# Gated-delta layer: the scan's matmuls laid over the whole TensorE array, and its reciprocal roots taken with GpSimd's power operation

## The chip, the cores and the metric

One core of one Trainium2 chip runs the whole program. The metric is the device time of one execution in microseconds (us). The core has a matrix engine (TensorE, PE in the profile, with PEld for its weight loads), VectorE (DVE), ScalarE (ACT), GpSimd (POOL), and queues that issue DMAs (SP is SyncE's). Each engine has a list of its own instructions and takes them in that order.

## The reference, cut to what matters

Two layers run over 1024 prompt frames and 64 sample frames (1088 columns, 17 chunks of 64). The first is a gated convolution with band attention and is not touched. The second is a gated DeltaNet with 8 heads of width 128. For each chunk it computes

```
def l2norm(x):
    return x * lax.rsqrt(jnp.sum(x * x, axis=-1, keepdims=True) + EPS)
...
u = sol[..., :HD_C] - jnp.einsum('bhlk,bhkv->bhlv', sol[..., HD_C:], S)
qk = jnp.einsum('blhd,bmhd->bhlm', q, k) * decay
o = jnp.einsum('blhk,bhkv->blhv', q * jnp.exp(gc)[..., None], S) + jnp.einsum('bhlm,bhmv->blhv', qk, u)
S_new = jnp.exp(g_last)[..., None, None] * S + jnp.einsum('blhk,bhlv->bhkv', k_dec, u)
```

S is a 128x128 state per head. It goes from chunk to chunk, so the chunks of a head are a chain. sol comes from a triangular solve inside the chunk and does not need S. The output o is normalized per head by the reciprocal root of its mean square, multiplied by silu(z) and projected.

## The kernel before

Heads are worked on in four pairs p = 0 to 3. The 64 rows of a chunk of one head of the pair lie in partitions 0 to 63, those of the other in 64 to 127. A pair's 17 chunks go in three batches of 6, 6 and 5. For each batch there are these steps:

- `prepare` (L947) transposes k and q of each chunk on TensorE (tile `tr`), squares and sums them on ScalarE (L976, `junk`), takes the reciprocal roots `rr` of the sums on VectorE by a bit trick and three Newton steps (`rsqrt`, L773), scales with them (`sT`, `sA`, `kap`, L985 to L987), and reads the products of k with k and of k with q out of PSUM into `An` and `KQD` (L997, L998). `kt` is a copy of the transposed k, `kd` that k times a decay.
- `substitute` (L1010) inverts 16x16 blocks on GpSimd in 28 small operations (`px`, `AL`) between two DMAs through DRAM; `join` (L1030) brings the blocks together with 32-wide matmuls; `solve` (L1098) writes the solved values over v (`vt`) and over k (in `kq`).
- `scan` (L1124) is the chain over chunks. Per chunk it makes `ks`, the products of k and of q with S; adds v to give `us`; makes `su`, the product of `kd` with `us`; updates S (L1185); and in `outputs` (L1132), one chunk later, makes the product of `KQD` with `us`, adds the q part (`qs`, L1173) and sums squares.
- `finish` (L1196) takes the reciprocal root for up to four chunks of output, with three VectorE operations before it, two for the bit trick and twelve GpSimd operations for Newton, and one VectorE operation behind (L1200 to L1204); it scales the outputs (L1206), transposes and stores them to DRAM.

Beside this chain TensorE runs the layer's projections: `pjt`, 128x384 or 128x320, three matmuls for each block of 128 rows because operands are split into a high and a low part (`project`, L175). For pairs 0 to 2 these are the projections and convolutions of the next pair; during the last pair's scan they are the eight gate tiles (`gate`, L847); then comes the output projection `out`.

TensorE's order is written by hand. Each step is a generator that issues its matmuls and then yields a waiting time in estimated ns; `Order.run` (L88) keeps an estimated clock, moved on by every matmul (`mm`, L115), and always takes the ready step of best rank, scan first and the projections last. The other engines' orders come from the tile framework's scheduler. PSUM tiles `tr` and `su` have two banks each, `ks` one. The layout that the change touches is `kq`: the pair's k of both heads, then its q of both, as [2, 17, 2, 64] in the free dimension (`new_kq`, L833). Each float32 matmul is two records in the trace, a transpose or a `pjt` matmul one.

The 64-row operands make TensorE use parts of its array: `ks` is four matmuls of 64 output rows (trace: 128*64), `su` two with 64 contraction rows (64*128), the output two of 64*64. `pjt`, the transposes, and `solve` use all of it (128*128).

Of the kernel before, what the change touches and what calls it, by code (L numbers as in the profile page):

```python
# [107 lines left out]
class Net:  # L108
# [651 lines left out]
    def odd(self):  # L760
# [12 lines left out]
        def rsqrt(out, x, tmp, eng):  # L773
            dve.tensor_scalar(out.bitcast(I32), x.bitcast(I32), 1, None, ALU.logical_shift_right)
            dve.tensor_scalar(out.bitcast(I32), out.bitcast(I32), -1, 0x5F3759DF, ALU.mult, ALU.add)  # L775
            for _ in range(3):
                if eng is dve:
                    dve.scalar_tensor_tensor(tmp, out, -0.5, x, ALU.mult, ALU.mult)
                    dve.tensor_tensor(tmp, tmp, out, ALU.mult)
                    dve.scalar_tensor_tensor(out, tmp, 1.5, out, ALU.add, ALU.mult)  # L780
                else:
                    pool.tensor_tensor(tmp, out, out, ALU.mult)  # L782
                    pool.tensor_tensor(tmp, tmp, x, ALU.mult)
                    pool.tensor_scalar(tmp, tmp, -0.5, 1.5, ALU.mult, ALU.add)
                    pool.tensor_tensor(out, out, tmp, ALU.mult)

# [46 lines left out]
        def new_kq(p):  # L833
            KQ[p] = k1.tile([P, 2, NCH, 2, 64], F32, name="kq", tag="kq", bufs=2)
# [4 lines left out]
        def conv_dst(p, i):  # L839
            q = i % 2  # L840
            if i < 2:
                return 8 + 2 * p + q, KQ[p][:, 0, :, q, :]
            if i < 4:
                return 2 * p + q, KQ[p][:, 1, :, q, :]
            return 16 + 2 * p + q, V[p][:, :, q, :]
# [27 lines left out]
        def gates(ba):  # L873
            for n in ("beta", "egc", "dec", "gc"):
                G[n] = comp(n)
            beta, egc, dec, gc = (G[n] for n in ("beta", "egc", "dec", "gc"))
            buf = G["buf"] = k1.tile([P, NCH * P], F32, name="dbuf", tag="vt", bufs=2)
            x, ab, gg = (buf[:, 68 * i:68 * i + 68].rearrange("p (a c) -> p a c", c=NCH) for i in range(3))
# [22 lines left out]
            for j, c0 in enumerate((C_U, C_BD, C_H, C_H + 1)):  # L901
                w = cst[:, c0:c0 + P] if j < 2 else cst[:, c0:c0 + 1].broadcast_to([P, P])
                self.mm(ps[:, 68 * j:68 * j + 68], w, gf)
            gcf = gc.rearrange("p a c -> p (a c)")
# [5 lines left out]
            act.activation(egl.rearrange("p q a c -> p (q a c)"), ps[:, 136:272], AF.Exp)  # L910
            yield 1500
# [30 lines left out]
        def zeroed():  # L942
            for name, w in (("Cb", 32), ("BD", P)):
                Z[name] = self.kp.tile([P, NBM, w], F32, name=name)
                pool.memset(Z[name], 0.0)

        def prepare(p, b):  # L947
# [16 lines left out]
            ss = self.kp.tile([P, 2, NBM], F32, name="ss", tag="ss", bufs=2)[:, :, :nb]  # L964
            rr = self.kp.tile([P, 2, NBM], F32, name="rr", tag="rr", bufs=3)[:, :, :nb]
            tmp = self.kp.tile([P, 2, NBM], F32, name="rt", tag="rt", bufs=2)[:, :, :nb]
            junk = self.kp.tile([P, P], F32, name="junk", tag="junk", bufs=1)
            for i0 in range(0, nb, 4):
                m = min(4, nb - i0)
                for a in range(2):  # L970
                    ps = pst("tr").rearrange("p (c j) -> p c j", j=P)
                    for i in range(m):
                        c = c0 + i0 + i
                        self.tr(ps[:, i, :], kq[:, a, c].rearrange("p q t -> p (q t)"))
                    for i in range(m):
                        act.activation(junk, ps[:, i, :], AF.Square, accum_out=ss[:, a, i0 + i:i0 + i + 1])  # L976
                    if a == 0:
                        act.copy(out=kt[:, i0:i0 + m, :], in_=ps[:, :m, :])
                        dve.tensor_tensor(kd[:, i0:i0 + m, :], ps[:, :m, :],
# [384 lines left out]
```

## Time and profile before

| what | value |
|---|---|
| median of 3 runs | 1439.04 us (1437.8 to 1440.11) |
| the profiled execution's own time | 1441.69 us |
| its span, first to last instruction | 1439.9 us |
| ScalarE, share of the span | 676.3 us, 47% |
| second layer with scan and solve steps, from the first `tr` tile | from about 678 us |
| first and last `ks` matmul | 793.4 and 1287.4 us |
| mean granted TensorE clock | 0.982 of full |

The profile shows one execution. A group row gives busy time, mean ns of one record, then the idle time of the engine just before, with what ended it. A wait row gives who waited for whom: total us, how often, the longest. A timeline row gives start us, length us, the instruction and how many records are merged. TensorE's lengths overlap, since matmuls are pipelined: what one costs is read from the distance between starts.

### The profile page before, as it was taken

Reading aid. Unit: us, or ns where it says so; the run is one execution under the profiler, and the core shown is the slowest. Engines: PE = TensorE matmul, PEld = TensorE weight load, DVE = VectorE, ACT = ScalarE, POOL = GpSimd, SP = SyncE. Lnnn points to the kernel's source line nnn. Section 1 sums busy time; section 2 is a strip of 40 time slices with the busy share of each in tenths; the row PEclk is TensorE's granted clock in tenths of the full one; section 3 lists DMA queues with packets and bytes.
Section 4 is the critical chain, followed back from the end, with each engine's and each line's share of the span. In section 5 each row is a group of like instructions: output and inputs, shape, how many; then the busy total and the mean of one; then the engine's idle time right before and its main releaser. Section 6 shows DMA issues by size and latency. Waiting matters only on the chain. (4 is left out here: it accounts for less than half of the span.)

```text
span 1439.9 us, 28413 instructions
## 1 busy us (share of the span) xinstructions
PE 1367.9 (95%) x10600; PEld 1231.2 (86%) x10600; DVE 867.4 (60%) x2496; ACT 676.3 (47%) x1776; POOL 304.9 (21%) x805
## 2 busy tenths in 40 slices
PE   8999999999999999899889999999898989999996
PEld 6989998998999899788768777778786778889995
DVE  7675257237425754777787768666765765433554
ACT  7643345144334455676445554545443534333652
POOL 4001000000100014321235325140524151410222
PEclk9999999999999999999988999999999999999998
DMA  8403111210211274541433112121311142336753
GB/s 267 138 17 90 57 53 45 87 53 27 78 58 47 65 237 140 174 165 38 110 83 67 42 40 70 31 60 33 68 34 42 39 99 61 104 107 219 228 198 117
DMA packets 113834, 132.73 MB, mean 92 GB/s; under 512 B 35280, under 2 KB 80792, under 8 KB 113696
## 3 DMA queue, kind: packets, MB, share of 16 engines
q1 hardware_dynamic: 82448, 104.32, 24.8%
q10 hardware_dynamic: 31248, 26.60, 5.7%
q8 instruction: 83, 1.36, 0.4%
q14 instruction: 55, 0.45, 0.1%
HBM read 99.71 MB, written 34.31 MB: 93 GB/s over the span
## 5 line engine op out<-in xcount | busy, mean ns | idle before, releaser
L119 PE MATMUL pjt<-hhi,wlo 128*128 128x384 f32 (+1 forms) x1768 | 616.9, 349 | 2.8 <-DVE wlo L165 2.8
L119 PE MATMUL pjt<-hhi,whi 128*128 128x384 f32 (+1 forms) x1768 | 583.7, 330 | 10.0 <-ACT whi L164 4.8
L119 PE MATMUL pjt<-hlo,whi 128*128 128x384 f32 (+1 forms) x1768 | 575.9, 329 | 1.0 <-DVE hlo L418 0.9
L119 PEld LDWEIGHTS pjt<-hhi,wlo 128*128 128x128 f32 x1768 | 337.1, 191 | 27.0 <-issue 11.9
L119 PEld LDWEIGHTS pjt<-hhi,whi 128*128 128x128 f32 x1768 | 337.2, 191 | 16.6 <-ACT whi L164 5.8
L119 PEld LDWEIGHTS pjt<-hlo,whi 128*128 128x128 f32 x1768 | 335.5, 190 | 1.9 <-DVE hlo L418 1.9
L165 DVE TENSOR_TENSOR wlo<-wf,whi 128x512 fp32r<-128x512 f32 x222 | 152.5, 710 | 165.4 <-ACT whi L164 164.1
L164 ACT CAST whi<-wf 128x512 fp32r<-128x512 f32 x222 | 130.1, 619 | 166.9 <-PE pjt L119 122.4
L639 ACT ACTIVATE pr<-pr,mx 128x640 f32<-128x640 f32 (+5 forms) x72 | 50.9, 707 | 89.4 <-DVE mx L638 88.8
L811 DVE SCALAR_TENSOR_TENSOR kq<-pjt,par,kq 128x384 f32<-128x384 f32 (+2 forms) x144 | 71.6, 497 | 2.9
L600 POOL MEMSET bias<- 64x64 f32 x8 | 1.5, 182 | 320.7 <-DMA bias<-Gd 295.5
L375 POOL TENSOR_TENSOR sqa<-sqa,sq 128x384 f32<-128x384 f32 (+1 forms) x36 | 39.9, 1109 | 138.0 <-ACT sq L372 137.9
L636 DVE CUSTOM_DVE_ANT_0 pr<-sc,bias 128x640 f32<-128x640 f32 (+5 forms) x72 | 47.9, 666 | 26.8 <-PE sc L119 25.9
L1022 POOL TENSOR_TENSOR px<-AL 48x14 f32<-48x14 f32 (+6 forms) x168 | 46.1, 274 | 61.0 <-DMA AL<-Sd 52.0
L1185 DVE SCALAR_TENSOR_TENSOR S<-S,egl,su 128x128 f32<-128x128 f32 x128 | 40.6, 342 | 30.0 <-PE su L119 29.6
L782 POOL TENSOR_TENSOR so<-so 128x4 f32<-128x4 f32 (+2 forms) x72 | 17.1, 238 | 176.0 <-DVE so L775 117.6
L976 ACT ACTIVATE junk<-tr 128x128 f32<-128x128 f32 x136 | 37.7, 277 | 34.0 <-PE tr L124 28.9
L1023 POOL TENSOR_TENSOR AL<-AL,px 48x14 f32<-48x14 f32 (+6 forms) x168 | 46.2, 275 | 9.4
L124 PE MATMUL pt<-cst,pr 128*128 128x128 f32 (+1 forms) x280 | 43.3, 270 | 4.4 <-DVE pr L641 2.9
L1144 ACT ACTIVATE junk<-o 128x128 f32<-128x128 f32 x68 | 21.0, 309 | 50.8 <-DVE o L1140 40.9
L119 PE MATMUL pjt<-mhi,whi 128*128 128x384 f32 x128 | 43.0, 336 | 1.1 <-ACT whi L164 1.1
L119 PE MATMUL pjt<-mhi,wlo 128*128 128x384 f32 x128 | 43.0, 336 | 0.5 <-DVE wlo L165 0.5
(257 smaller groups left out, 2192.0 us busy)
## 6 DMA issues: line engine op xcount, KB each, us to landing
wf<-in_w_in SPq DMA_DIRECT2D x128, 256.0 KB, 3.7
wf<-in_w_out SPq DMA_DIRECT2D x96, 256.0 KB, 3.2
mf<-mixd SPq DMA_DIRECT2D x31, 192.0 KB, 4.5
x<-in_x SPq DMA_DIRECT2D x8, 384.0 KB, 5.8
xg<-in_x SPq DMA_DIRECT2D x2, 1536.0 KB
xd<-xg SPq DMA_DIRECT2D x2, 1536.0 KB
Dd<-dbuf ACTq DMA_DIRECT2D x16, 192.0 KB, 3.6
od<-o ACTq DMA_DIRECT2D x12, 256.0 KB, 2.3
```

The lines of the kernel that those rows point to most:

```text
L119: return self.pe.matmul(out, lhsT=lhsT, rhs=rhs, start=start, stop=stop, **k)
L124: return self.pe.transpose(out, in_, self.ident[0:k, 0:k])
L164: self.act.copy(out=hi, in_=x)
L165: (eng or self.dve).tensor_tensor(lo, x, hi.bitcast(F32), ALU.subtract)
L375: pool.tensor_tensor(acc, acc, sq, ALU.add)
L636: dve.tensor_tensor_reduce(out=cut(pr[0:nq, :nk]), in0=sc[0:nq, :nk // nw, :nw], in1=cut(b["bias"][a][0:nq, j0:j0 + nk]), scale=1.0, scala ...
L639: act.activation(pr[0:nq, :nk], pr[0:nq, :nk], AF.Exp, bias=mx[0:nq, 1:2], scale=1.0, accum_out=mx[0:nq, 2:3])
L811: dve.scalar_tensor_tensor(oi, ch(ps[:, i0 + j + 1:i0 + j + 1 + m]), cw[j], oi, ALU.mult, ALU.add)
L976: act.activation(junk, ps[:, i, :], AF.Square, accum_out=ss[:, a, i0 + i:i0 + i + 1])
L1022: pool.tensor_tensor(t, AL[:, j + 1:16, j:j + 1].broadcast_to([lanes, m, w]), x.broadcast_to([lanes, m, w]), ALU.mult)
L1023: pool.tensor_tensor(o, o, t, ALU.add)
L1185: dve.scalar_tensor_tensor(Sn[:, q, :], S[:, q, :], egl[:, q, p, c:c + 1], su[q], ALU.mult, ALU.add)
```

## The change

`kq` becomes [17, 4, 64]: per chunk k of head 0, q of head 0, q of head 1, k of head 1. So one head's k and q lie side by side, and head 0 has k in the lower half while head 1 has k in the upper half. From this follows:

- `ks` is one matmul per head with 128 output rows (k rows and q rows together), two in place of four.
- `u0` and `u1` are two fixed tiles [128, 2, 128], zeroed once. Head q's 64 rows are written in its own half and its own column block, and the other half stays zero. `su` is then one matmul with 128 contraction rows and 256 columns in place of two.
- Adding v is two VectorE operations on 64 partitions in place of one on 128. The q part is copied by two ScalarE operations straight into `o4` in place of one into `qs`. In a pair's first chunk, where there is no S, two copies fill `u` (before, `vt` was used itself).
- The product of `KQD` with `u` is issued in the same chunk, right behind `su`, and its halves come out swapped (tile positions (0, 64) and (64, 0)); `finish` takes that into account, and a second copy of the factor exp(gc) with swapped halves (`egs`) is made once in `gates` with two small matmuls.
- The yields in `scan` are 1050 in place of 850 behind `ks`, and 700 behind the first chunk's copies.
- In `prepare` the transposes are per head, `kt` is copied in two 64-partition pieces, and `kd` is made from `kt` in SBUF instead of from PSUM.
- The roots: GpSimd adds EPS (two operations) and raises to -0.5 with one `pow` operation per batch; VectorE makes `eq`, EPS times the q sum. `finish` is one GpSimd add and one GpSimd `pow`; its VectorE operations before and behind the root go.

The core of the diff (renamed access patterns in `conv_dst`, `solve` and `finish`, and the two matmuls and one exponential for `egs` are left out):

```diff
-            KQ[p] = k1.tile([P, 2, NCH, 2, 64], F32, name="kq", tag="kq", bufs=2)
+            KQ[p] = k1.tile([P, NCH, 4, 64], F32, name="kq", tag="kq", bufs=2)
...
-                    if a == 0:
-                        act.copy(out=kt[:, i0:i0 + m, :], in_=ps[:, :m, :])
-                        dve.tensor_tensor(kd[:, i0:i0 + m, :], ps[:, :m, :],
-                                          dec[:, p, c0 + i0:c0 + i0 + m].unsqueeze(2).broadcast_to([P, m, P]), ALU.mult)
+                    h = slice(64 * q, 64 * q + 64)
+                    act.copy(out=kt[h, i0:i0 + m, :], in_=ps[h, :m, :])
                     yield 2160
-            dve.tensor_scalar(ss, ss, EPS, None, ALU.add)
-            rsqrt(rr, ss, tmp, dve)
...
+                dve.tensor_tensor(kd[:, i0:i0 + m, :], kt[:, i0:i0 + m, :],
+                                  dec[:, p, c0 + i0:c0 + i0 + m].unsqueeze(2).broadcast_to([P, m, P]), ALU.mult)
+            for q in range(2):
+                h, o = slice(64 * q, 64 * q + 64), slice(64 - 64 * q, P - 64 * q)
+                pool.tensor_scalar(rk[h], sx[h, q, :], EPS, None, ALU.add)
+                dve.tensor_scalar(eq[o], sx[o, q, :], EPS, 128.0 * EPS, ALU.add, ALU.mult)
+            pool.tensor_tensor(rk, rk, Z["root"].broadcast_to([P, nb]), ALU.pow)
+            dve.tensor_tensor(sT, beta[:, p, c0:c0 + nb], rk, ALU.mult)
...
-                    for a in range(2):
-                        for q in range(2):
-                            self.mm(ks[64 * q:64 * q + 64, P * a:P * a + P], kq[:, a, c, q, :], S[:, q, :], share=1.6)
-                    u = self.kp.tile([P, P], F32, name="us", tag="us", bufs=2)
-                    dve.tensor_tensor(u, ks[:, 0:P], vt[:, c, :], ALU.add)
-                    qs = self.kp.tile([P, P], F32, name="qs", tag="qs", bufs=2)
-                    act.activation(qs, ks[:, P:2 * P], AF.Copy, scale=egc[:, p, c:c + 1])
-                    yield 850
+                    for q in range(2):
+                        self.mm(ks[:, col[q]], kq[:, c, 2 * q:2 * q + 2, :].rearrange("p a t -> p (a t)"), S[:, q, :])
+                    for q in range(2):
+                        dve.tensor_tensor(u[half[q], q, :], ks[half[q], col[q]], vt[half[q], c, :], ALU.add)
+                    for q in range(2):
+                        o = half[1 - q]
+                        act.activation(o4[o, a, :], ks[o, col[q]], AF.Copy, scale=egs[o, p, c:c + 1])
+                    yield 1050
...
-                    su.append(pst("su")[:, 0:P])
-                    self.mm(su[q], kd[h, i, :], u[h])
+                su = pst("su")[:, 0:2 * P]
+                self.mm(su, kd[:, i, :], u.rearrange("p q j -> p (q j)"))
...
+                o = pst("tr")[:, 0:P]
+                for q in range(2):
+                    self.mm(o[half[1 - q]], KQD[half[q], i, :], u[half[q], q, :], share=1.6, tile_position=(64 * q, 64 - 64 * q))
+                if S is not None:
+                    dve.tensor_tensor(o4[:, a, :], o, o4[:, a, :], ALU.add)
...
-            dve.scalar_tensor_tensor(va, va, 1.0 / (128.0 * 128.0), rq, ALU.mult, ALU.mult)
-            dve.tensor_tensor(va, va, rq, ALU.mult)
-            dve.tensor_scalar(va, va, EPS, None, ALU.add)
-            rsqrt(fa, va, tm, pool)
-            dve.scalar_tensor_tensor(fa, fa, 128.0 ** -0.5, rq, ALU.mult, ALU.mult)
+            pool.tensor_tensor(fa, so[:, 0, :m], R[p, b]["eq"][:, i0:i0 + m], ALU.add)
+            pool.tensor_tensor(fa, fa, Z["root"].broadcast_to([P, m]), ALU.pow)
```

TensorE's order over one chunk of the last pair's scan, before. `tr<-us,KQD` is the previous chunk's output, and the rows named `pjt` are projections that fill the time; x is a count of matmuls.

```order
L119 MATMUL tr<-us,KQD 64x128 x2
L119 MATMUL ks<-S,kq 64x128 x4
L119 MATMUL pjt<-hhi_6049,wlo 128x384
L119 MATMUL pjt<-hhi_6049,whi 128x384
L119 MATMUL pjt<-hlo_6050,whi 128x384
L119 MATMUL pjt<-hhi_6049,wlo 128x384
L119 MATMUL pjt<-hhi_6049,whi 128x384
L119 MATMUL pjt<-hlo_6050,whi 128x384
L119 MATMUL su<-us,kd 128x128 x2
```

The same engine over a chunk of the same scan, after the change.

```order
L119 MATMUL ks<-S,kq 128x128 x2
L119 MATMUL pjt<-hhi_6049,wlo 128x384
L119 MATMUL pjt<-hhi_6049,whi 128x384
L119 MATMUL pjt<-hlo_6050,whi 128x384
L119 MATMUL pjt<-hhi_6049,wlo 128x384
L119 MATMUL pjt<-hhi_6049,whi 128x384
L119 MATMUL pjt<-hlo_6050,whi 128x384
L119 MATMUL pjt<-hhi_6049,wlo 128x384
L119 MATMUL pjt<-hhi_6049,whi 128x384
L119 MATMUL pjt<-hlo_6050,whi 128x384
L119 MATMUL su<-u_7067,kd 128x256
L119 MATMUL tr<-u_7067,KQD 64x128 x2
```

The output's product moved from ahead of `ks` to right behind `su`, `ks` stands alone between full-array projections, and nine projections instead of six lie between `ks` and `su`.

VectorE before, around the second batch of the second pair, from the second Newton step to the reads of PSUM (`vt<-pjt` rows are the convolution of v, `rt` and `rr` the root).

```order
L778 SCALAR_TENSOR_TENSOR rt<-rr,ss 128x12
L811 SCALAR_TENSOR_TENSOR vt<-pjt,par,vt 128x6x64
L779 TENSOR_TENSOR rt<-rt,rr 128x12
L780 SCALAR_TENSOR_TENSOR rr<-rt,rr 128x12
L985 TENSOR_TENSOR sT<-beta,rr 128x6
L987 SCALAR_TENSOR_TENSOR kap<-egc,rr 128x6
L986 SCALAR_TENSOR_TENSOR sA<-sT,rr 128x6
L997 SCALAR_TENSOR_TENSOR An<-tr,sA,Dst 128x64 x4
L998 TENSOR_TENSOR KQD<-tr,DT 128x256
```

The same place after the change; `rk` is the root that comes from GpSimd.

```order
L977 TENSOR_SCALAR eq<-sx 64x6
L971 TENSOR_TENSOR kd<-kt,dec 128x256
L1163 SCALAR_TENSOR_TENSOR S<-S,egl,su 128x128 x2
L1171 TENSOR_TENSOR o_9279<-tr,o_9279 128x128
L789 MEMSET pjt 128x3
L797 SCALAR_TENSOR_TENSOR vt<-pjt,par,vt 128x6x64
L979 TENSOR_TENSOR sT<-beta,rk 128x6
L981 SCALAR_TENSOR_TENSOR kap<-egc,rk 128x6
L797 SCALAR_TENSOR_TENSOR vt<-pjt,par,vt 128x6x64
L980 SCALAR_TENSOR_TENSOR sA<-sT,rk 128x6
L797 SCALAR_TENSOR_TENSOR vt<-pjt,par,vt 128x6x64
L992 SCALAR_TENSOR_TENSOR An<-tr,sA,Dst 128x64 x4
```

The Newton steps are gone from VectorE, and `sT`, which needs GpSimd's root, stands in the row with convolution, `An` and `KQD` behind it. GpSimd for the same batch, before, inside the substitution of the batch ahead:

```order
L1022 TENSOR_TENSOR px<-AL 48x56
L1023 TENSOR_TENSOR AL<-AL,px 48x8x7
L1022 TENSOR_TENSOR px<-AL 48x56
L1023 TENSOR_TENSOR AL<-AL,px 48x7x8
L1022 TENSOR_TENSOR px<-AL 48x54
L1023 TENSOR_TENSOR AL<-AL,px 48x6x9
```

After the change:

```order
L1017 TENSOR_TENSOR px<-AL 48x56
L1018 TENSOR_TENSOR AL<-AL,px 48x8x7
L1017 TENSOR_TENSOR px<-AL 48x56
L976 TENSOR_SCALAR rk<-sx 64x6
L1018 TENSOR_TENSOR AL<-AL,px 48x7x8
L978 TENSOR_TENSOR rk<-rk,root 128x6
L1017 TENSOR_TENSOR px<-AL 48x54
L1018 TENSOR_TENSOR AL<-AL,px 48x6x9
```

The root now stands on GpSimd between the substitution's operations, which begin only when the DMA of `AL` has landed.

More of the change, by code (lines that the diff above doesn't have):

```diff
@@ L873, in gates @@
         def gates(ba):
-            for n in ("beta", "egc", "dec", "gc"):
+            for n in ("beta", "egc", "egs", "dec"):
                 G[n] = comp(n)
-            beta, egc, dec, gc = (G[n] for n in ("beta", "egc", "dec", "gc"))
+            beta, egc, dec = (G[n] for n in ("beta", "egc", "dec"))
             buf = G["buf"] = k1.tile([P, NCH * P], F32, name="dbuf", tag="vt", bufs=2)
+            gc = G["gc"] = buf[:, 1600:1668].rearrange("p (a c) -> p a c", c=NCH)
             x, ab, gg = (buf[:, 68 * i:68 * i + 68].rearrange("p (a c) -> p a c", c=NCH) for i in range(3))
@@ L982, in prepare @@
-            dve.tensor_scalar(ss, ss, EPS, None, ALU.add)
-            rsqrt(rr, ss, tmp, dve)
-            sT, sA, kap = small("sT"), small("sA"), small("kap")
-            dve.tensor_tensor(sT, beta[:, p, c0:c0 + nb], rr[:, 0, :], ALU.mult)
-            dve.scalar_tensor_tensor(sA, sT, -1.0, rr[:, 0, :], ALU.mult, ALU.mult)
-            dve.scalar_tensor_tensor(kap, egc[:, p, c0:c0 + nb], -1.0, rr[:, 0, :], ALU.mult, ALU.mult)
+                        act.activation(junk, ps[:, i, :], AF.Square, accum_out=sx[:, q, i0 + i:i0 + i + 1])
@@ L1127, in scan @@
             kd, KQD = rr["kd"], rr["KQD"]
-            egc, egl = G["egc"], G["egl"]
+            egs, egl = G["egs"], G["egl"]
             vt = V[p].rearrange("p c q t -> p c (q t)")
+            half = [slice(0, 64), slice(64, P)]
+            col = [slice(0, P), slice(P, 2 * P)]
             S = state.get(p)
-            def outputs(i, o4, so, u, qs):
-                o = pst("tr")[:, 0:P]
-                for q in range(2):
-                    h = slice(64 * q, 64 * q + 64)
-                    self.mm(o[h], KQD[h, i, :], u[h], share=1.6, tile_position=(64 * q, 64 * q))
-                a = i % 4
-                if qs is not None:
-                    dve.tensor_tensor(o4[:, a, :], o, qs, ALU.add)
-                else:
-                    dve.tensor_copy(o4[:, a, :], o)
-                junk = self.kp.tile([P, P], F32, name="junk", tag="junk", bufs=1)
-                act.activation(junk, o4[:, a, :], AF.Square, accum_out=so[:, 0, a:a + 1])
-                if a == 3 or i == nb - 1:
-                    order.add(f"fin{p}.{b}.{i - a}", 3, finish(p, b, i - a, a + 1, o4, so), [])
-            last = None
             for i in range(nb):
-                if i % 4 == 0:
+                c, a = c0 + i, i % 4
+                if a == 0:
                     if len(fins) > 2:
@@ L1184, in scan @@
                     if S is not None:
-                        dve.scalar_tensor_tensor(Sn[:, q, :], S[:, q, :], egl[:, q, p, c:c + 1], su[q], ALU.mult, ALU.add)
+                        dve.scalar_tensor_tensor(Sn[:, q, :], S[:, q, :], egl[:, q, p, c:c + 1], su[:, col[q]], ALU.mult, ALU.add)
                     else:
-                        dve.tensor_copy(Sn[:, q, :], su[q])
+                        dve.tensor_copy(Sn[:, q, :], su[:, col[q]])
+                o = pst("tr")[:, 0:P]
+                for q in range(2):
+                    self.mm(o[half[1 - q]], KQD[half[q], i, :], u[half[q], q, :], share=1.6, tile_position=(64 * q, 64 - 64 * q))
+                if S is not None:
+                    dve.tensor_tensor(o4[:, a, :], o, o4[:, a, :], ALU.add)
+                else:
+                    dve.tensor_copy(o4[:, a, :], o)
                 S = Sn
-                last = i, o4, so, u, qs
+                junk = self.kp.tile([P, P], F32, name="junk", tag="junk", bufs=1)
+                act.activation(junk, o4[:, a, :], AF.Square, scale=128.0 ** -0.5, accum_out=so[:, 0, a:a + 1])
+                if a == 3 or i == nb - 1:
+                    order.add(f"fin{p}.{b}.{i - a}", 3, finish(p, b, i - a, a + 1, o4, so), [])
                 yield 1110
-            outputs(*last)
             if b == NB - 1:
```

67 lines of the change are left out of this document (26 added, 41 removed).

## The prediction

> **What bounds the kernel now.** I read the page's first part, then the windows by stage, then the matrix engine's waits, and last its timeline over single chunks.
>
> ```profile
> span 1439.9 us, 28413 instructions
> PE 1367.9 (95%) x10600; PEld 1231.2 (86%) x10600; DVE 867.4 (60%) x2496; ACT 676.3 (47%) x1776; POOL 304.9 (21%) x805
> ```
>
> TensorE is busy 95% of the span; no other engine passes 60%. The windows say whether that holds where the change is. Their columns are the stretch, its length, then busy us of PE, PEld, DVE, ACT and POOL, the granted TensorE clock, the DMA share and GB/s.
>
> ```profile
> 0.00:678.00 678.00, 659.64 (x4306) 616.97 (x4308) 387.60 (x957) 330.29 (x728) 76.13 (x84) 1.00 0.30 97
> 678.00:790.00 112.00, 95.90 (x739) 86.83 (x737) 85.16 (x220) 57.56 (x152) 45.18 (x88) 0.91 0.32 83
> 790.00:1310.00 520.00, 498.14 (x4902) 417.15 (x4901) 328.58 (x1211) 225.89 (x769) 156.86 (x608) 0.98 0.25 61
> 1310.00:1440.00 130.00, 114.19 (x663) 110.20 (x661) 66.06 (x109) 62.56 (x129) 26.75 (x25) 0.96 0.60 197
> ```
>
> The scan runs from 790 to 1310. There TensorE idles 520.00 - 498.14 = 22 us, under 5%. So in this stage a microsecond off TensorE's work is a microsecond off the span, unless it turns into a wait. From 678 to 790, before the scan, it idles 16 us and the clock was granted at 0.91: there the other engines bind. The change touches only the roots there.
>
> ```profile
> PE tr L124 <- DVE KQD L998: 5.8, 4, 3.4
> PE tr L119 <- DVE KQD L998: 4.6, 6, 3.3
> PE su L119 <- DVE us L1171: 4.0, 2, 2.7
> POOL px L1022 <- DMA AL<-Sd: 52.0, 12, 9.8
> ```
>
> The first two rows are TensorE waiting for a PSUM bank that VectorE empties behind the roots, 10.4 us. The third is the scan itself waiting for VectorE, only twice. The fourth is GpSimd waiting for a DMA, at present at nobody's cost on TensorE's path.
>
> **TensorE's work in the scan, the main term.** Timeline rows of the last pair, then a `solve` group and a `decays` group that use the whole array:
>
> ```profile
> 1228.94 0.34 PE L119 MATMUL pjt<-hlo,whi 128*128 128x384 f32 x1
> 1229.21 0.49 PE L119 MATMUL su<-us,kd 64*128 64x128 f32 x4
> 1229.63 0.44 PE L119 MATMUL pjt<-hhi,wlo 128*128 128x384 f32 x1
> 1229.91 0.34 PE L119 MATMUL pjt<-hhi,whi 128*128 128x384 f32 x1
> ...
> 1235.62 0.34 PE L119 MATMUL pjt<-hlo,whi 128*128 128x384 f32 x1
> 1235.89 0.43 PE L119 MATMUL tr<-us,KQD 64*64 64x128 f32 x4
> 1236.26 0.66 PE L119 MATMUL ks<-S,kq 128*64 128x128 f32 x8
> 1236.85 0.44 PE L119 MATMUL pjt<-hhi,wlo 128*128 128x384 f32 x1
> 1237.13 0.34 PE L119 MATMUL pjt<-hhi,whi 128*128 128x384 f32 x1
> ...
> 1237.82 0.34 PE L119 MATMUL pjt<-hlo,whi 128*128 128x384 f32 x1
> ```
>
> ```profile
> 1085.42 0.34 PE L119 MATMUL pjt<-hlo,whi 128*128 128x384 f32 x1
> 1085.60 0.60 PE L119 MATMUL tr<-vr,BD 128*128 128x128 f32 x4
> 1085.96 0.42 PE L119 MATMUL pjt<-hhi,wlo 128*128 128x384 f32 x1
> 1086.22 0.34 PE L119 MATMUL pjt<-hhi,whi 128*128 128x384 f32 x1
> ...
> 701.62 0.34 PE L119 MATMUL pjt<-hlo,whi 128*128 128x384 f32 x1
> 701.79 0.70 PE L119 MATMUL tr<-dbuf,cst 128*128 128x320 f32 x2
> 702.09 0.58 PE L119 MATMUL pjt<-hhi,wlo 128*128 128x384 f32 x1
> 702.50 0.33 PE L119 MATMUL pjt<-hhi,whi 128*128 128x384 f32 x1
> ```
>
> From 1237.13 to 1237.82 lie four projections, 0.1725 us each. I price a group as the distance from the projection ahead of it to the second projection behind it, less two such slots (0.345), because the first projection behind is late too.
>
> - `su`: 1229.91 - 1228.94 - 0.345 = 0.625. Its own part, 1229.21 to 1229.63, is 0.42; so 0.205 goes to entering and leaving, 0.10 for each change between whole array and part of it.
> - Output and `ks` together: 1237.13 - 1235.62 - 0.345 = 1.165. Own parts 0.37 and 0.59, again 0.205 for the two changes. Between the two, 64*64 and then 128*64, there is none.
> - Two whole-array matmuls of 128 columns (`tr<-vr,BD`, four records): 1086.22 - 1085.42 - 0.345 = 0.455. They start 0.18 behind the projection: no entry price.
> - One of 320 columns: 702.50 - 701.62 - 0.345 = 0.535. An estimate for 256 columns, on the line between 0.455 / 2 = 0.23 and 0.535: 0.43.
>
> The new `ks` has the shape of `tr<-vr,BD`: 0.455 for 0.59, over 64 chunks 8.6 us saved. The new `su` costs 0.43 for 0.42, over 68 chunks 0.7 us lost. The output stays 64*64; the crossed positions are taken at the same 0.37. Changes between whole and part of the array, counted along the two orders over the second layer, are 374 before and 252 after: each chunk keeps only the output's, often shared with a neighbouring small group. 122 x 0.10 = 12.2 us saved. Sum: 8.6 - 0.7 + 12.2 = 20.1 us. The two matmuls for `egs` cost a tenth of a microsecond.
>
> [...]
>
> **The other engines, none on the path as I see it.**
>
> ```profile
> L1171 DVE TENSOR_TENSOR us<-ks,vt 128x128 f32<-128x128 f32 x64 | 18.3, 286 | 12.5 <-PE ks L119 12.0
> L1173 ACT ACTIVATE qs<-ks,egc 128x128 f32<-128x128 f32 x64 | 23.5, 368 | 24.8 <-DVE us L1171 23.1
> L978 ACT COPY kt<-tr 128x512 f32<-128x512 f32 (+2 forms) x24 | 10.9, 456 | 0.0
> L779 DVE TENSOR_TENSOR rt<-rt,rr 128x12 f32<-128x12 f32 (+1 forms) x36 | 8.1, 226 | 0.4
> L1200 DVE SCALAR_TENSOR_TENSOR so<-so,rr 128x4 f32<-128x4 f32 (+2 forms) x24 | 3.8, 158 | 3.6 <-ACT junk L1144 3.3
> L782 POOL TENSOR_TENSOR so<-so 128x4 f32<-128x4 f32 (+2 forms) x72 | 17.1, 238 | 176.0 <-DVE so L775 117.6 <-DVE rt L779 36.5 <-DVE rr L780 19.2
> L988 POOL TENSOR_TENSOR kt<-kt,kap 128x768 f32<-128x768 f32 (+1 forms) x12 | 16.8, 1401 | 58.1 <-DVE sA L986 56.8 <-DVE kap L987 1.3
> ```
>
> VectorE loses 12 small operations per batch (12 x 12 x 0.226 = 32.5 us) and 6 per `finish` (24 x 6 x 0.158 = 22.8). It gains a second `u` operation per chunk (64 x 0.286 = 18.3, since I let half the partitions cost as much), 8 first copies at the same price (2.3) and 24 for `eq` (3.8). Net about 31 us less. ScalarE gains 64 x 0.368 + 24 x 0.456 = 34.5 us, bringing it to some 711 us, half the span. `kd` from SBUF is taken as unchanged: it is needed only in the scan, behind the substitution.
>
> The chain from `ks` to `su` gets one VectorE operation longer, 0.29 us. Six projections covered it, 6 x 0.1725 = 1.04 us; in the commonest place it is now nine, 1.55. If that cover is gone, 0.29 us per chunk, at most 64 x 0.29 = 18.6 us. The output's product waits for the same `u` as `su`, so its move adds no wait. What queues behind the second `u` is the update of S, which `ks` of the next chunk waits for, again with projections between. Stores of outputs start a chunk earlier and are waited for by no one in the scan.
>
> The power operation is in no row. Its floor is a small GpSimd operation, 0.24 us. The nearest row above is all that it replaces on GpSimd, twelve such, 2.9 us; `kt`'s 1.40 us for 768 columns says that 4 to 6 columns are not long by size. I take 1 us, between the two. A batch's root is now two adds and a power, 2 x 0.24 + 1 = 1.5 us, against 12 x 0.226 = 2.7 us on VectorE: no later than before, and `sT`, which waits for it, holds up no one. Up to a power of 2.2 us this stays so.
>
> **The rivals.**
>
> - Roots late because the power is long (slower). `sT` stands in VectorE's row, behind it `An` and `KQD`, which free TensorE's PSUM banks; that TensorE waits here is shown by the 10.4 us. Each us over 2.2 costs up to 12 us over 12 batches. From 2.2 + 20.1 / 12 = 3.9 us the whole gain is gone; at 5.4 us it is 12 x 3.2 = 38 us, 1457. For it: a power is no simple operation. Against: four to six columns. Chance 0.11.
> - Roots late because of their place. In a pair's second batch they stand on GpSimd inside the substitution, which waits for a DMA, 52.0 / 12 = 4.3 us each. Four pairs: 17 us, 1436. Against: VectorE's own row then also runs later. Chance 0.07.
> - The longer chain from `ks` to `su` is covered in half the chunks only: 9.3 us, 1428. For it: some chunks have no projections between; against: the third wait row, twice in 64. Chance 0.12.
> - The 128-row matmuls do not take away the entering and leaving: gain 7.9, 1431. Against: `tr<-vr,BD` shows neither. Chance 0.05.
> - The four 64-column `ks` overlap in pairs so far that, outside the chunk shown, they take no longer than two whole ones: the 8.6 us go, 1427.6. Against: 0.59 us against 0.455. [...] Chance 0.04.
> - The roots' relief also ends the waits for `KQD`, 10.4 us more: 1408.6. For it: VectorE has 2.7 us less ahead of each. Against: half of these waits may be PSUM reads themselves. Chance 0.14.
>
> **How the numbers follow.** The sum is a difference, so I set it against the median, 1439.04; the profiled execution took 1441.69, 0.2% more, with a span of 1439.9. 1439.0 - 20.1 = 1419, chance 0.47. The range goes from the sixth case to the second, 1408 to 1436; outside lie the long power and the edges, together under 0.2. About 0.2%, 3 us, is what a measurement here can tell from no change. Within it lies half of the second case, 0.04; slower, 0.11; faster, the rest, 0.85.
>
> **What would show it.** Right: `ks` as two 128*128 matmuls, 0.45 us from start to leaving with no entry step; `su` 0.43; only the output still 64*64; VectorE near 836 us, ScalarE near 711; TensorE's idle time from 790 to the scan's end still near 22 us. Wrong: power rows over 2 us with `sT` waiting for GpSimd and TensorE for `KQD`; `su` waiting for `u` in many chunks; a step ahead of the new `ks`. If the time falls by far less than 20 us while TensorE's groups cost what is said here, the waits are what I missed.

## The result, and the profile after

The change made the kernel slower: 1452.16 us median of 4 runs (1451.69 to 1453.34) against 1438.42 for the kernel before on the same chip (4 runs, 1436.86 to 1440.11). The ratio is 1.0084, 95% interval 1.0062 to 1.0105, some 12 us. The forecast was 1419 with a range up to 1436, so it was wrong in sign.

The first part of the page of after:

```profile
span 1449.9 us, 27378 instructions
PE 1361.3 (94%) x10212; PEld 1247.1 (86%) x10212; DVE 856.8 (59%) x2304; ACT 711.5 (49%) x1865; POOL 292.9 (20%) x604
```

The span grew by 10.0 us while TensorE's busy time fell by 6.6 (1367.9 to 1361.3). So TensorE's time without work grew by 16.6, from 72.0 to 88.6. And 6.6 is not the 20 us that the forecast took off. Here are two places of the last pair's scan in the timeline of after, one at `su`, one at `ks`:

```profile
1281.80 0.34 PE L119 MATMUL pjt<-hlo,whi 128*128 128x384 f32 x1
1281.98 0.59 PE L119 MATMUL su<-u,kd 128*128 128x256 f32 x2
1282.50 0.43 PE L119 MATMUL tr<-u,KQD 64*64 64x128 f32 x4
1282.87 0.44 PE L119 MATMUL pjt<-hhi,wlo 128*128 128x384 f32 x1
1283.15 0.33 PE L119 MATMUL pjt<-hhi,whi 128*128 128x384 f32 x1
...
1284.38 0.33 PE L119 MATMUL pjt<-hlo,whi 128*128 128x384 f32 x1
1284.55 0.61 PE L119 MATMUL ks<-S,kq 128*128 128x128 f32 x4
1284.92 0.42 PE L119 MATMUL pjt<-hhi,wlo 128*128 128x384 f32 x1
1285.17 0.34 PE L119 MATMUL pjt<-hhi,whi 128*128 128x384 f32 x1
```

By the rule with which the forecast priced a group, `su` and output cost 1283.15 - 1281.80 - 0.345 = 1.005 us; it had said 0.43 + 0.37 + 0.205 = 1.005. `ks` costs 1285.17 - 1284.38 - 0.345 = 0.445; it had said 0.455, with no step ahead of it. So the groups are as cheap as forecast. The saving is real, and what eats it lies between the groups. TensorE's waits of after, from 690 to 1300, the largest:

```profile
PE tr L119 <- DVE XT L1047: 14.9, 3, 8.3
PE tr L119 <- ACT kt L969: 7.0, 9, 1.3
PE tr L119 <- DVE KQD L993: 6.8, 2, 4.1
PE tr L124 <- DVE o L1190: 6.3, 2, 3.8
PE su L119 <- DVE u L1149: 5.4, 4, 2.6
PE tr L124 <- DVE dbuf L921: 5.2, 3, 2.9
PE tr L124 <- DVE KQD L993: 3.6, 5, 1.3
```

Six of the seven rows are matmuls into a `tr` tile that wait for an input (`XT`, the `o` of `finish`) or for the readers of an earlier `tr` tile (`kt`, `KQD`, `dbuf`). The row on `XT` grew most. Before, it was:

```profile
PE tr L119 <- DVE XT L1070: 0.8, 1, 0.8
```

But it stays between 12.6 and 18.6 us in three kernels below that are about 20 us faster than the change (e6, e9, e13), so it is not what these gain back. The waits for `KQD` are 10.4 us, as they were before. The other 13.5 us of the missing gain (20.1 - 6.6) are in busy time, and the windows around the longest wait show that the work behind it took longer. Columns as in the windows of before; the third number from the end, ahead of the DMA share, is the granted clock.

```profile
770.00:778.00 8.00, 0.99 (x6) 0.67 (x4) 3.90 (x10) 4.35 (x7) 2.88 (x11) 0.76 0.34 90
778.00:781.00 3.00, 1.68 (x51) 1.65 (x52) 0.97 (x3) 0.24 (x1) 2.35 (x10) 0.50 0.01 2
781.00:784.00 3.00, 3.00 (x56) 2.53 (x55) 0.75 (x3) 0.00 (x0) 2.33 (x9) 0.50 0.00 0
784.00:787.00 3.00, 3.00 (x38) 2.71 (x37) 1.18 (x4) 0.62 (x2) 2.37 (x9) 0.93 0.02 5
```

The 8.3 us wait ends at 779.3. Up to about 784.4 (the 0.93 of the last row is 0.4 us at half) the clock is granted at 0.50, and projections follow each other every 0.32 us in place of 0.173, as in these two timeline rows:

```profile
780.57 0.52 PE L119 MATMUL pjt<-hhi,whi 128*128 128x384 f32 x1
780.89 0.52 PE L119 MATMUL pjt<-hlo,whi 128*128 128x384 f32 x1
```

This wait thus cost its own length and some 2.6 us more (half of 5.1), an estimate from these rows. Over the execution the mean clock was 0.973 after and 0.982 before: 0.9% of 1440 us, an estimate of 13 us, about the 13.5 us of that busy time.

### The profile page after: what moved, and what is told of

Its sections match the earlier page's. It is cut to its first block, busy times and chain, and to the rows that moved or that the text cites. A ratio compares the mean times of both kernels' runs of the same rounds, so it can differ in the third digit from the quotient of the medians.

```text
span 1449.9 us, 27378 instructions
## 1 busy us (share of the span) xinstructions
PE 1361.3 (94%) x10212; PEld 1247.1 (86%) x10212; DVE 856.8 (59%) x2304; ACT 711.5 (49%) x1865; POOL 292.9 (20%) x604
## 5 line engine op out<-in xcount | busy, mean ns | idle before, releaser
L119 PEld LDWEIGHTS pjt<-hhi,whi 128*128 128x128 f32 x1768 | 339.6, 192 | 15.7 <-ACT whi L164 6.1
L1152 ACT ACTIVATE o<-ks,egs 64x128 f32<-64x128 f32 x128 | 46.4, 362 | 52.0 <-DVE u L1149 41.6
L1149 DVE TENSOR_TENSOR u<-ks,vt 64x128 f32<-64x128 f32 x128 | 36.8, 287 | 38.7 <-PE ks L119 37.2
L124 PE MATMUL pt<-cst,pr 128*128 128x128 f32 (+1 forms) x280 | 43.4, 270 | 4.4 <-DVE pr L641 2.9
L119 PE MATMUL su<-u,kd 128*128 128x256 f32 x136 | 42.2, 392 | 5.4 <-DVE u L1149 5.4
```

The costliest lines, as they stand in the source:

```text
L119: return self.pe.matmul(out, lhsT=lhsT, rhs=rhs, start=start, stop=stop, **k)
L124: return self.pe.transpose(out, in_, self.ident[0:k, 0:k])
L1152: act.activation(o4[o, a, :], ks[o, col[q]], AF.Copy, scale=egs[o, p, c:c + 1])
```

## The experiments

All ratios are to the kernel before on the same chip, with 95% intervals; differences between kernels are differences of ratios times 1440 us. "The change" is 1.0084.

| run | what it is | median us | ratio to before |
|---|---|---|---|
| e1 | change, Newton roots | 1465.48 | 1.0131 (1.0089 to 1.0173) |
| e2 | before, power roots | 1451.41 | 1.0050 (1.0023 to 1.0076) |
| e3 | change, a waiting time in `norm` 850 | 1456.44 | 1.0080 (1.0059 to 1.0100) |
| e4 | change, `ks` in four parts | 1463.24 | 1.0146 (1.0119 to 1.0173) |
| e5 | change, `kt` copied by VectorE | 1464.98 | 1.0162 (1.0133 to 1.0192) |
| e6 | change, output late | 1434.64 | 0.9942 (0.9919 to 0.9966) |
| e7 | change, yields a tenth longer | 1445.76 | 1.0026 (1.0009 to 1.0042) |
| e8 | before, output early | 1468.35 | 1.0163 (1.0100 to 1.0226) |
| e9 | change, output in its own bank | 1436.84 | 0.9950 (0.9924 to 0.9976) |
| e10 | e9, add one chunk later | 1439.05 | 0.9966 (0.9943 to 0.9988) |
| e11 | e6, Newton roots | 1453.16 | 1.0056 (1.0033 to 1.0079) |
| e12 | e9, `ks` in four parts | 1456.39 | 1.0092 (1.0072 to 1.0111) |
| e13 | change, three `tr` banks | 1435.26 | 0.9938 (0.9908 to 0.9967) |
| e14 | before, output in the `ks` bank | 1470.26 | 1.0187 (1.0160 to 1.0215) |
| e15 | e13, yields a tenth longer | 1438.79 | 0.9973 (0.9958 to 0.9987) |
| e16 | e13, Newton roots | 1454.73 | 1.0072 (1.0045 to 1.0100) |
| e17 | e13, Newton for k only | 1433.31 | 0.9931 (0.9903 to 0.9958) |
| e18 | e13, Newton in `finish` only | 1443.40 | 0.9990 (0.9973 to 1.0008) |

### First: roots, and the distance from ks to su (e1, e2, e3)

e1 puts the Newton steps back into the changed kernel. Its `finish` keeps the change's GpSimd add ahead of the Newton steps, so it stands in GpSimd's row twice, before and behind VectorE's bit trick; the kernel before entered it once.

```diff
-                pool.tensor_scalar(rk[h], sx[h, q, :], EPS, None, ALU.add)
+                dve.tensor_scalar(ex[h], sx[h, q, :], EPS, None, ALU.add)
...
-            pool.tensor_tensor(rk, rk, Z["root"].broadcast_to([P, nb]), ALU.pow)
+            rsqrt(rk, ex, et, dve)
...
-            pool.tensor_tensor(fa, fa, Z["root"].broadcast_to([P, m]), ALU.pow)
+            rsqrt(fa, va, tm, pool)
```

> The changed kernel with only the roots undone: Newton steps on VectorE per batch and on GpSimd per group of four chunks, as before; scan, layout and TensorE's order stay those of the change. Theory 1 (the roots on GpSimd are late and TensorE pays for it): the 20 us of TensorE work come through, about 1420 us, and the waits for XT and KQD fall to about the 10 us of before. Theory 2 (the scan's own longer chain and ScalarE's extra copies cost it): about 1448 to 1452 us, as with the change.

e2 makes only the roots of the kernel before with the power:

```diff
-            dve.tensor_scalar(ss, ss, EPS, None, ALU.add)
-            rsqrt(rr, ss, tmp, dve)
+            for a in range(2):
+                pool.tensor_scalar(rr[:, a, :], ss[:, a, :], EPS, None, ALU.add)
+                pool.tensor_tensor(rr[:, a, :], rr[:, a, :], Z["root"].broadcast_to([P, nb]), ALU.pow)
...
-            rsqrt(fa, va, tm, pool)
+            pool.tensor_tensor(fa, va, Z["root"].broadcast_to([P, m]), ALU.pow)
```

> The kernel before with only the roots changed: one GpSimd add and one power of 6 columns for k, then the same for q (two powers per batch where the change has one), and one power in place of Newton per group of chunks. Theory 1: slower than before by 20 us or more, about 1460 us, with VectorE's sT waiting for the root and TensorE for XT. Theory 2: within 5 us of before, 1434 to 1443 us.

e3 was meant to put the yield behind `ks` back. Its edit changed another yield of the same value, the one in `norm` (L332); the one behind `ks` (L1153) stayed at 1050:

```diff
                     pool.tensor_tensor(acc, acc, sq, ALU.add)
-            yield 1050
+            yield 850
```

> The change with the waiting time behind ks back at 850, so that mostly six projections instead of nine lie between ks and su. Theory 1: no more than 3 us either way from the change. Theory 2: if the chain over chunks in TensorE's order is what lasts too long, 5 to 10 us faster than the change; if the longer chain on VectorE needs the cover, 5 to 10 us slower, with su waiting for u in more than the 4 places.

e1 is 1.0131: without the power the changed kernel is no better, so the roots alone are not the cause. e2 is 1.0050, some 7 us, its ten runs spread from 1441.68 to 1459.06: the power roots alone cost the old kernel a little. The profile, of the slowest of these runs, shows where TensorE waits for them:

```profile
PE tr L119 <- DVE XT L1054: 16.4, 3, 11.2
```

e3 tested neither of its theories. In its trace the projections between `ks` and `su` are the same as in the change, nine in 32 of the 64 chunks. So whether the longer yield costs anything stays open; it is in e6, e9 and e13 too and does not keep them from being faster. Most of what loses the gain is in the scan or the layout, though the roots do matter there (below).

### Second: where in the scan (e4 to e7)

e4 makes `ks` in four matmuls of 64 output rows; the estimated clock is moved on as by two whole ones, so TensorE's order stays:

```diff
-                        self.mm(ks[:, col[q]], kq[:, c, 2 * q:2 * q + 2, :].rearrange("p a t -> p (a t)"), S[:, q, :])
+                        t = self.order.now
+                        for j in range(2):
+                            self.mm(ks[half[j], col[q]], kq[:, c, 2 * q + j, :], S[:, q, :])
+                        self.order.now = t + (128 * 4 / 2.4 / 1 + 3)
```

> The change with each head's ks made again by two matmuls of 64 output rows (four per chunk), in the same TensorE order. It gives TensorE back 64 x (0.59 + 0.205 - 0.446) = 22 us of work at most (fewer where a small group stands next to it). Theory A, TensorE's work sets the time in the scan, as the forecast had it: 12 to 22 us slower than the change. Theory W, the time is set by chains on the other engines, which are waited for at fixed places of the order, so that work taken off TensorE comes back as waiting: within 4 us of the change, and its waits shrink by about what its work grows.

e5 is one line in `prepare`:

```diff
-                    act.copy(out=kt[h, i0:i0 + m, :], in_=ps[h, :m, :])
+                    dve.tensor_copy(kt[h, i0:i0 + m, :], ps[h, :m, :])
```

> The change with the two half copies of kt made by VectorE in place of ScalarE, so that a transpose bank is no longer held by four squares and a copy one after the other on ScalarE. Theory B, the banks held by ScalarE cost the gain: the 7.9 us of waits for kt go, with what the clock loses behind them 8 to 12 us faster than the change. Theories W and the roots: within 4 us of the change.

e6 moves the output back to one chunk later, all else as in the change:

```diff
+                if last:
+                    outputs(*last)
                 if S is not None:
...
-                o = pst("tr")[:, 0:P]
...
+                last = i, o4, so, u, S is not None
```

> The change with the product of KQD and u, and what follows it, issued one chunk later, ahead of the next ks, as in the kernel before. Theory P, the early output costs the gain, because its transpose bank waits for VectorE's add, which stands behind the update of S and ScalarE's copy: the waits for o go, 5 to 12 us faster than the change. Theories W, B and the roots: within 4 us.

e7 multiplies the yields of the second layer's steps by 1.1 (`STEPS` stands here for the list of the beginnings of their names):

```diff
-                t[4] = self.now + w
+                t[4] = self.now + w * (1.1 if t[2][:3] in STEPS else 1)
```

> The change with every waiting time of the scan's, solve's, join's, substitution's, prepare's and finish's steps a tenth longer, so that more projections stand between a step and the one that needs its result. Theory W: the waits for XT, KQD and o shrink, 5 to 15 us faster than the change. If the waits are held by something else than distance (banks, VectorE's load): no faster, within 4 us or slower.

e6 is the find: 0.9942, 20 us faster than the change and 8 faster than before (1.0084 - 0.9942 = 0.0142). Theory P named the right part, but 5 to 12 us and not 20; by which mechanism is open after this. e5 makes things worse by 11 us: theory B falls. TensorE's wait for `kt` stays, now for VectorE, and one wait for `KQD` reaches 6.9 us:

```profile
PE tr L119 <- DVE KQD L993: 9.7, 2, 6.9
PE tr L119 <- DVE kt L969: 9.2, 8, 2.1
```

e7 gains 8 us. e4 lies between its theories: up to 22 us of work given back cost 9.

### Third: what the early output takes (e8 to e11)

e8 is the kernel before with `outputs` called in its own chunk:

```diff
-                if last:
-                    outputs(*last)
...
-                last = i, o4, so, u, qs
+                outputs(i, o4, so, u, qs)
```

> The kernel before with one part of the change alone: the product of KQD and us issued in its own chunk, right behind su, with its add and square. Theory P, the early output is by itself what costs the gain: 10 to 20 us slower than before. Rival: it costs only together with the new layout: within 4 us of before.

e9 leaves the output early and gives it a PSUM bank, taken from `su`, which needs one tile per chunk now where it had two:

```diff
-            return self.pg.tile([P, 512], F32, name=tag, tag=tag, bufs=2 if tag in ("tr", "su") else 1)
+            return self.pg.tile([P, 512], F32, name=tag, tag=tag, bufs=2 if tag == "tr" else 1)
...
-                o = pst("tr")[:, 0:P]
+                o = pst("ob")[:, 0:P]
```

> The change with the early output in a PSUM bank of its own in place of one of the two tr banks (su gives up one of its two); TensorE's order is the same. Theory P-bank, the early output keeps a tr bank that prepare, join and solve need: 10 to 20 us faster than the change, near the kernel with the late output. Theory P-order, it is the place of the output and what follows it in the engines' rows: within 5 us of the change.

e10 adds to e9 that the add and the square are emitted ahead of the next `u`:

```diff
-                    dve.tensor_tensor(o4[:, a, :], o, o4[:, a, :], ALU.add)
...
+                last = i, o4, so, o, S is not None
...
+                if last:
+                    outputs(*last)
```

> The kernel with the output's own bank, its product still right behind su, but VectorE's add and ScalarE's square one chunk later, ahead of the next u. Theory P-vector, VectorE's add behind the update of S is what is in the way (VectorE then waits at the head of its row for the next ks): 10 to 20 us faster than the kernel with the own bank alone. Theory P-order on TensorE: within 5 us of that kernel, and still slower than the late output.

e11 is e6 with e1's roots.

> The late output with the reciprocal roots made by Newton steps again (VectorE for k, GpSimd in finish), so only the layout of the change is left. Theory: the roots on GpSimd cost the layout's gain a part, by the waits for XT (12.6 us in the late kernel): 5 to 13 us faster than the late output. Rival: the late output has room for the roots too: within 4 us of it.

e8 is decisive for the move: alone, in the old kernel, it costs 23 us (1.0163, interval 14 to 33 us). Not all of that need be the bank: the largest row of its profile is `PE tr L124 <- DVE o L1202: 14.8, 4, 10.0`, the scaled outputs of `finish`, against 4.5 us before. e9 is decisive for how: with the output just as early and TensorE's order the same, a bank of its own brings 19 us (1.0084 to 0.9950). e10 is no faster than e9, so with a bank of its own VectorE's place for the add is not in the way. Theory P-bank stands. The same four groups in both kernels show it. After:

```profile
814.86 0.70 PE L119 MATMUL su<-u,kd 128*128 128x256 f32 x2
815.49 0.43 PE L119 MATMUL tr<-u,KQD 64*64 64x128 f32 x4
817.15 0.63 PE L124 MATMUL tr<-cst,vt 128*128 128x128 f32 x4 [1.22 <-DVE KQD L993]
818.29 1.01 PE L119 MATMUL tr<-BD,kt 128*128 128x128 f32 x4 [0.52 <-DVE o L1171]
```

And e9, where the output's tile is `ob`:

```profile
813.53 0.70 PE L119 MATMUL su<-u,kd 128*128 128x256 f32 x2
814.16 0.44 PE L119 MATMUL ob<-u,KQD 64*64 64x128 f32 x4
814.53 0.66 PE L124 MATMUL tr<-cst,vt 128*128 128x128 f32 x4
815.82 1.13 PE L119 MATMUL tr<-BD,kt 128*128 128x128 f32 x8 [0.63 <-DVE KQD L993]
```

From `su` to the fourth group it is 3.43 us in the change and 2.29 in e9. In the change the output takes one of two banks. The next transposes then find the other still held by the products that `KQD` is read from, and those behind them find the output waiting for its add, which stands behind the update of S on VectorE. Only 0.52 us of that carries the output's name; the 1.22 us is charged to `KQD`. That is why no large wait row pointed at the output. It also goes the other way: the output's product waits for a bank, with all that stands behind it in TensorE's row.

```profile
887.71 0.44 PE L119 MATMUL tr<-u,KQD 64*64 64x128 f32 x4 [0.70 <-ACT kt L969]
```

e11 was a surprise, 16 us slower than e6 with the power, where 5 to 13 faster or the same was expected: in the new layout this variant of the Newton roots costs, in the old one (e2) the Newton steps did not.

### Fourth: banks, work and roots (e12 to e18)

e12 is e9 with e4's four matmuls:

> The output's own bank, with each head's ks made by two matmuls of 64 output rows again, in the same TensorE order: up to 22 us of TensorE work given back. Theory A', with the bank free TensorE's work sets the time: 12 to 22 us slower than the own bank alone. Theory W, chains of the other engines set it even then: within 5 us.

e13 gives the free bank to `tr` and leaves the output there:

```diff
-bufs=2 if tag in ("tr", "su") else 1
+bufs=3 if tag == "tr" else 1
```

> The change with three tr banks and one su bank, the early output in a tr bank as in the change, TensorE's order the same. Theory P-bank, the number of banks is what is short: 10 to 25 us faster than the change, at least as fast as the own bank. Rival: the own bank gained by something else than the number of tr banks (VectorE's row came out otherwise): within 5 us of the change.

e14 writes the late output of the kernel before beside `ks`:

```diff
-                o = pst("tr")[:, 0:P]
+                o = ks[:, 2 * P:3 * P]
```

> The kernel before with its late output written beside ks in the ks bank, in place of a tr bank. If the tr banks bind the kernel before as well: 4 to 12 us faster than before, so that a part of what the own bank gave was not the change's. If the late output keeps a tr bank too short to matter: within 4 us.

e15 is e13 with e7's longer yields:

> Three tr banks and every waiting time of the steps a tenth longer, the version to beat both. If the two gains are of different waits they add: about 8 us faster than three banks alone, near 1425. If the longer distances only avoided the short bank: within 4 us of three banks alone.

e16 is e13 with e1's roots; e17 takes of them only k's, e18 only `finish`'s.

> Three tr banks and all reciprocal roots by Newton steps as before: the layout of the change alone, with the bank short no longer. Theory A', layout and roots are independent and the layout's 20 us come through: 12 to 20 us faster than before. Rival, as the late output with Newton steps showed (10 us slower than before): the new layout needs the lighter roots, 10 to 20 us slower than three banks with the power.

> Three tr banks, k's roots by Newton steps on VectorE, finish's roots by the power. If finish's twelve small GpSimd operations and VectorE's five are what the power pays for: within 4 us of three banks with both powers, or faster by the waits for XT. If k's twelve VectorE operations are: 10 to 20 us slower.

> The other half: three tr banks, k's roots by the power, finish's roots by Newton steps on GpSimd. If finish's roots are what the power pays for: 8 to 20 us slower than three banks with both powers. If k's are: within 4 us.

e13 settles the bank: a third one is worth 21 us (1.0084 to 0.9938), at least as much as the own bank. TensorE's order is the same, instruction by instruction, in the change, e9 and e13, and these are TensorE's waits of e13 for `kt` and `KQD`:

```profile
PE tr L119 <- ACT kt L969: 1.8, 4, 0.7
PE tr L124 <- DVE KQD L993: 1.5, 1, 1.5
PE tr L119 <- DVE KQD L993: 0.6, 1, 0.6
```

Together these are 3.9 us. In the change the same waits, with the output's add, come to 20.3 us: the three rows shown above and three smaller ones of 2.9. The late output with three banks was not run, so whether a third bank would help that kernel as well is open. e15 is no faster than e13, so what e7 gained is not there once the banks are enough.

e12 against e9 tests the forecast's main claim. The first lines of e9 and then of e12:

```profile
span 1436.0 us, 27423 instructions
PE 1355.4 (94%) x10212; PEld 1244.4 (87%) x10212; DVE 856.8 (60%) x2304; ACT 711.3 (50%) x1865; POOL 295.2 (21%) x604
```

```profile
span 1453.7 us, 27937 instructions
PE 1372.8 (94%) x10468; PEld 1239.3 (85%) x10468; DVE 858.5 (59%) x2304; ACT 712.7 (49%) x1865; POOL 293.5 (20%) x604
```

With the bank free, TensorE's busy time grows by 17.4 us and the span by 17.7; by the ratios it is 20 us (0.9950 to 1.0092). With the bank short the same edit cost 9 (e4), and there the busy time itself grew by only 9.8 us (1361.3 to 1371.1). The time without work stayed about the same (88.6 and 87.1), and the granted clock went up from 0.973 to 0.979. So "a microsecond of TensorE's work is a microsecond of the span" is about true of the scan once PSUM is not short. Each of the two differences, 20 and 9, is uncertain by some 5 us, an estimate from the intervals.

e14 was not the test that it was meant to be. It is 27 us slower than before, by a wait that the edit itself brought:

```profile
PE ks L119 <- DVE o L1140: 29.0, 49, 2.4
```

With both products in one tile, `ks` now waits 49 times for the add of the output. Whether the kernel before is short of banks stays open.

The roots, on three banks: both powers 0.9938, Newton for k 0.9931, Newton in `finish` 0.9990, both Newton 1.0072. With the power in `finish`, k's root may be either. Where `finish` uses Newton steps, its scaled outputs come late and the transposes wait for them. TensorE's waits of e13, of e17 and then of e18, the rows on that and, of the last two, the longest:

```profile
PE tr L124 <- DVE o L1190: 8.0, 2, 4.6
```

```profile
PE tr L119 <- DVE XT L1063: 17.0, 3, 7.7
...
PE tr L124 <- DVE o L1206: 1.3, 1, 1.3
```

```profile
PE tr L124 <- DVE o L1205: 18.9, 4, 8.4
PE tr L119 <- DVE XT L1062: 14.3, 2, 10.6
```

`o` is the scaling in `finish`: 8.0 us with both powers (e13), 1.3 with the power in `finish` alone (e17) and 18.9 with Newton steps there (e18). Since this Newton variant enters GpSimd's row twice, the figure holds for it, not for the old `finish`. e1, e11, e16 and e18 therefore say that the power in `finish` helps against this variant, not what the layout is worth alone.

e17 and e13 are the fastest kernels found, 0.7% and 0.6% faster than before; their intervals overlap almost entirely, and those of e6 and e9 overlap with them.

## Why the prediction was wrong, point by point

- **TensorE's groups, 20.1 us: right, group by group.** `ks` 0.445 for 0.455, `su` with output 1.005 as said, no entry step at `ks`. In e13, whose matmuls are the same, TensorE's busy time is 1349.2 us, 18.7 less than before; 15.1 of that lie between the first and the last `ks`.
- **"The output's product waits for the same `u` as `su`, so its move adds no wait": this step failed.** It looked at the product's inputs and not at its output. The product is written to a `tr` bank, one of two that `prepare`, `join`, `solve` and `finish` also need. Ahead of `ks` the bank was freed by VectorE's next operation; behind `su` it is freed behind the update of S. Price: 23 us by the move alone (e8, a part of it perhaps in `finish`), 19 to 21 us got back by a bank (e9, e13) or by moving it back (e6).
- **"A microsecond off TensorE's work is a microsecond off the span, unless it turns into a wait": right in the condition, wrong in leaving it there.** Up to 22 us of work cost 20 with the bank free and 9 with the bank short (e12, e4).
- **TensorE's idle time from 790 to the scan's end "near 22 us": wrong.** Between the first and the last `ks` it was 34.3 us; in e13, with the third bank, it is 22.6. It was the sign named for the case that "the waits are what I missed", and it came out so. The clock's share was not in the sum: the mean granted clock was 0.973 after and 0.982 before, and 0.50 behind the longest wait.
- **"The change touches only the roots" from 678 to 790: this failed too, by 8 us that the third bank does not give back** (table below).
- **The rivals.** The slower side was given to the roots, by their length or their place. The length did not happen: the power took 1.35 us, under the 2.2 us from which it was to cost. `sT` did wait for GpSimd, 14.5 us in total, but TensorE's waits for `KQD` stayed at 10.4 us; so the sixth rival, that they go, did not happen either. The place did happen in GpSimd's row: the substitution of a pair's first batch grew from 15.5 to 25.5 us in the first pair and from 9.4 to 11.1 us to about 13.8 in the others. In the old layout e2 shows the same growth in the first pair (25.4 us) and is 7 us slower than before. In the new one the price of the place is not shown: e17, without k's root on GpSimd, is as fast as e13, and its wait for `XT` is still 17.0 us. The chain from `ks` to `su` showed 5.4 us of waits for `u`, against 4.0 before: hardly a rival. The two rivals on small matmuls fell: no entry step stands ahead of the new `ks`, and four `ks` cost more than two (e12, 20 us). No rival had the output itself holding a PSUM bank.
- **VectorE "near 836 us": 856.8; ScalarE "near 711": 711.5.** VectorE's 192 instructions fewer are as counted. The durations of all its instructions sum to 25.2 us less (981.9 to 956.7), near the 31 forecast. Busy time counts overlapping records once and fell by 10.6 only: part of the removed small steps lay beside others.

What stays open: with enough banks the kernel is 8 to 9 us faster than before, not 20. In e13's profile TensorE's busy time is down by 18.7 us, and the rest of the span went up from 72.0 to 82.9. The stages show where. Each cell has the length and TensorE's idle time in it, in us:

| stage | before | after | e13 |
|---|---|---|---|
| up to the first `tr` tile | 677.8, 18.4 | 676.2, 17.4 | 676.0, 18.1 |
| from there to the first `ks` | 115.6, 16.1 | 126.1, 21.9 | 123.7, 24.7 |
| from the first to the last `ks` | 494.0, 21.9 | 495.7, 34.3 | 479.7, 22.6 |
| behind the last `ks` | 152.5, 15.7 | 151.9, 15.0 | 152.7, 17.6 |

In the scan the change with the third bank is 14.3 us faster, for 15.1 us less busy time and the idle time of before. The 15.1 are 5 us short of the 20.1; the granted clock, 0.975 in this stage of e13 and 0.983 before, accounts by estimate for 3.7 of them (0.8% of 457). Ahead of the scan 8.1 us are lost, and there stands the longest part of e13's largest wait:

```profile
PE tr L119 <- DVE XT L1047: 18.6, 3, 11.5
```

This is the start of `join`, behind the substitution on GpSimd and its two DMAs; the wait of 11.5 us is the first batch's. In e13 that substitution takes 21.8 us where it took 15.5 before, with the next batch's root between its steps. But in e17, without k's root there, it takes 18.4 us and the stage is 124.5 us long. So what costs these 8 us stays open; no run shortened that chain.

## What to carry to other kernels

When an operation is moved, list what it holds as well as what it needs: here a product issued earlier took its PSUM bank earlier, and with two banks in turn the wait appeared under whoever held the other one (1.22 us under `KQD` and 0.52 under the output, in the rows of after from 814.86). So a full bank rotation is looked for by giving one consumer a bank of its own with the order unchanged, not by reading the wait rows. And a TensorE that was 95% busy gave back the work taken off it only with enough banks between its groups: with the early output the scan, 494.0 us before, took 495.7 with two `tr` banks (after) and 479.7 with three (e13). A freed bank was worth about the same to the tile with most users (e13, 21 us) as to the output alone (e9, 19 us).

## What the runs showed of the hardware

- TensorE's granted clock was halved behind some of its waits. In after it was 0.50 from within the wait of 8.3 us until about 784.4 (rows above), and also behind some shorter waits; here are the windows behind a wait of 2.47 us that ended at 873.2 and one of 2.73 us that ended at 1021.1:

```profile
873.20:875.20 2.00, 2.00 (x16) 1.70 (x18) 0.05 (x1) 0.62 (x2) 0.00 (x0) 0.50 0.00 0
875.20:877.20 2.00, 2.00 (x13) 1.50 (x9) 1.38 (x6) 0.17 (x1) 0.00 (x0) 0.65 0.23 66
...
1021.10:1023.10 2.00, 2.00 (x20) 1.79 (x20) 1.87 (x8) 0.93 (x5) 0.41 (x1) 1.00 0.21 70
```

Behind the first the clock was 0.50, behind the second, which was longer, 1.00. So between these two the length alone did not decide it; what did is not shown.

- GpSimd's power is not a small operation but no long one either, in the groups of after:

```profile
L1188 POOL TENSOR_TENSOR so<-so,root 128x4 f32<-128x4 f32 (+2 forms) x24 | 20.4, 849 | 1.3
L978 POOL TENSOR_TENSOR rk<-rk,root 128x6 f32<-128x6 f32 (+1 forms) x12 | 16.2, 1350 | 0.7
```

Taken apart by shape, the mean is 634 ns for 1 column, 700 for 2, 1019 for 4, 1290 for 5 and 1380 for 6, against 238 ns of a simple operation (L782 of before): in these groups it grows with the columns, but is not proportional to them.

- VectorE's add of v takes 287 ns on 64 partitions (L1149) and took 286 on 128: in this operation half the partitions cost as much as all of them, as the forecast had assumed.
